# Recurrence gates with the two halves of the split input stacked over the rows of a 64-channel block: two products per block instead of three per gate

## The chip, the cores and the metric

The kernel runs on one core of a Trainium2 chip. The metric is the device time of one execution in microseconds (us), the median of several runs. TensorE multiplies matrices: a product (MATMUL) sends the columns of its moving operand through an array that holds the weights, and each product has a weight load (LDWEIGHTS) of its own ahead of it. ScalarE (ACT in the profile) does activations and casts, VectorE (DVE) the arithmetic on two operands, GpSimd (POOL) little here, SyncE (SP) issues DMAs. Each engine takes its instructions in the order of the program.

## The reference, cut to what matters

Two layers of a mixed backbone over 256 latent and 256 context tokens, with three token mixers in each layer, a merge by gates and an MLP. The change lies in the first mixer, a bidirectional gated linear recurrence whose two gates are products with block-diagonal weights (eight blocks of 64 channels):

```python
xc = centred_depthwise_conv(x_in, conv_w, conv_b).astype(F32)
xb = xc.reshape(B, T, LRU_BLOCKS, LRU_BLOCK)              # 8 blocks of 64
r = sigmoid(einsum('btni,dnio->dbtno', xb, wa) + ba)      # d: two directions
i = sigmoid(einsum('btni,dnio->dbtno', xb, wx) + bx)
log_a = -LRU_C * r * softplus(-lam)
a = exp(log_a)
b = sqrt(-expm1(2.0 * log_a)) * (i * xc)
hf = linear_scan(a[0], b[0], h0f, False)
hb = linear_scan(a[1], b[1], h0b, True)
y = (hf + hb) * gelu(gate_in)
```

## The kernel before

Activations are held feature-major: 128 channels in the partitions, up to 512 tokens in the columns. Every float32 product is made from three products in the type float32r: weights and input are split into a rounded high part and a low rest (`split`, L223: a copy on ScalarE, a subtraction on VectorE), and high times high, high times low and low times high are summed in PSUM. Nearly all of TensorE's work is such triples on streamed weights (`mm3`, L234, and L1027 to L1029 for the products called ptok). ScalarE and VectorE split each piece of weights (whi and wlo) ahead of its use, with four buffers each.

Between these streamed products, `Lanes` issues the steps of dependent chains: H (the second mixer, `hgrn`), A (attention), L (the recurrence, `lru`), N (norms) and X (modulation). A step is what a chain does up to its next `yield`; the numbers that it yields (VectorE's time and a delay) decide when the next step is issued. The tile framework's scheduler then lays the issued work out on each engine, and the result is a fixed order of instructions per engine.

`lru` runs once for each of four heads j (128 channels, so two blocks of 64) in each of two layers: eight times. It splits the gates' weights (gw into lw) and the convolved input (xc into lx), then for each direction d makes the two gates: `pr` (recurrence gate, its tanh into rr) and `pi` (input gate, its tanh into iis). The weights of one gate and direction are one 128x128 matrix with the two 64x64 blocks on its diagonal and zeros elsewhere. A gate is three products of 128 rows, 128 columns of weights and 512 tokens (L847), so `lru` has 12 products, and the kernel 96. Each gate's PSUM tile is of the tag "L", which has one buffer: the next gate's first product waits until the tanh has read the last one.

The other tiles that the text names are lv (products of the second mixer within blocks, L547), sc (attention scores, L746, where two heads of 64 rows each lie side by side in the array), tp (transposes, L793), pav (attention output, L812), pg (the merge's gates, through `mm3`), PT, s and sog (results on ScalarE of the attention and of the second mixer's output gate), ge (the gelu of the recurrence's other branch).

Of the kernel before, what the change touches and what calls it, by code (L numbers as in the profile page):

```python
# [10 lines left out]
F32 = mybir.dt.float32  # L11
# [5 lines left out]
ALU = mybir.AluOpType  # L17
# [39 lines left out]
def merge_order(l):  # L57
    # some gates first, while the mixers' chains end
    count = {}
    for part in MERGE[l].split():  # L60
        bi = int(part[0])
        for what in part[1:]:
            i = count.get((bi, what), 0)
            count[bi, what] = i + 1
            yield bi, BRANCH_ORDER[bi], {"g": "gate", "p": "proj"}[what], i
# [35 lines left out]
class Piece:  # L101
    """Products with streamed weights: body(weights) yields after each run of products."""
# [5 lines left out]
class Lanes:  # L108
    """Chains of dependent steps that are issued between the runs of products.

    A step yields the time that the vector engine needs for what it issued, and how many runs more the chain waits."""
# [43 lines left out]
def hybrid_kernel(  # L155
# [67 lines left out]
    def split(hi, lo, src, scale=None, eng=nc.vector):  # L223
        # hi <- rounded part of scale * src, lo <- the rest
        if scale is None:
            nc.scalar.copy(hi, src)  # L226
            eng.tensor_tensor(out=lo, in0=src, in1=hi.bitcast(F32), op=ALU.subtract)  # L227
        else:
            nc.scalar.mul(hi, src, scale)
            nc.vector.scalar_tensor_tensor(  # L230
                out=lo, in0=src, scalar=scale, in1=hi.bitcast(F32), op0=ALU.mult, op1=ALU.subtract
            )
# [13 lines left out]
    def mm3_pairs(dsts, ws, x, nk, c0, c1):  # L246
        # two pieces at a time, so that x may still be arriving
# [15 lines left out]
    def layer_scalars():  # L263
# [13 lines left out]
        for l in range(DEPTH):  # L277
            # f = lb + (1 - lb) * (1 + tanh) / 2 as offset and slope
# [40 lines left out]
    def rope_tables(l):  # L319
        # ctab[:, cos|sin, tile, k|q, head, :], with the norm's gains and the scores' scale  # L320
# [8 lines left out]
    mod = [cpool.tile([P, 3, 2, 16], F32, name=f"mod{l}") for l in range(DEPTH)]  # L329

    def modulation_rows():
        # most sections, a row for each feature: the vector engine has time while the tensor engine is busy
# [34 lines left out]
    def last_modulation():  # L367
        # the last section: four groups of columns in four parts of the array
# [55 lines left out]
    def column_sums(parts, n, tag="A"):  # L424
        # sums over the features, one column for each 128 tokens
# [12 lines left out]
    def spread(r, n, tag="A"):  # L438
        # a row of n * 128 columns in every partition
# [14 lines left out]
    def modulated(u, r, a, b, k, s):  # L454
        # u = h * r * a + b in high and low parts
# [29 lines left out]
    def small_rstd(ss, n, temps):  # L485
        # 1 / sqrt(ss / n + eps) for a few columns: a first guess from the exponent, two steps
# [6 lines left out]
        # with x = v * r * r: r * (15 - 10 x + 3 x^2) / 8, but for the factor 3 / 8, then r * (3 - x) / 2 with that factor  # L493
# [14 lines left out]
    def first_half():  # L508
        # the latent stream's norm, before its products are issued
        q_ = lanes.lanes["N"]  # L510
        while len(q_) > 1 and lanes.step("N"):
            pass

# [1 line left out]
    def hgrn(l, j, TF, Q, vtok, sog, ys):  # L515
# [4 lines left out]
        # products over blocks, states of the context stream  # L520
# [9 lines left out]
        # within blocks of 64 tokens, the blocks of a tile side by side  # L530
# [7 lines left out]
        def place(b, src, shift):  # L538
            # blocks in the upper (b = 0) or the lower half of the partitions
# [13 lines left out]
        def mixed(t, hh, c0, n):  # L553
            # [first halves of slot 0 | second halves of slot 1] of the 2*hh blocks in columns c0..c0+n
# [17 lines left out]
        # A^T[s, t] of both directions, level by level  # L572
        Tt = TF[:]
        width = T2
        for lev in range(8):
# [11 lines left out]
            # widen the products to blocks of 2*hh  # L587
# [30 lines left out]
        # final states of the context stream  # L618
# [18 lines left out]
        # outputs, token-major  # L637
# [34 lines left out]
    def attention(l, j, qk, vtok, bias, ys):  # L672
        Tq = T2 if l == 0 else TL
        misc = two_k("misc")
        # normalised keys and queries, token-major: [k | q] of two heads for each 128 tokens
# [23 lines left out]
        # rotary embedding of the latent tokens  # L699
# [48 lines left out]
        def softmax(qt, sc):  # L748
            # both heads at once
# [55 lines left out]
        def applied(qt):  # L805
            # both heads at once, in two parts of the array
# [28 lines left out]
    def lru(l, j, xc, ge, gw, ys):  # L835
# [6 lines left out]
        split(*xs, xc)  # L842
        yield 1.2, 0

        def product(dst, i):
            for n, (a, b) in enumerate(((0, 0), (0, 1), (1, 0))):
                nc.tensor.matmul(dst, lhsT=ws[a][:, i, :], rhs=xs[b], start=(n == 0), stop=(n == 2))  # L847
        for d in range(2):
            c = 2 * j + d
            pr_ = psum("L", "pr")  # L850
            product(pr_, 2 * d)
            nc.scalar.activation(rr[:, d], pr_, AF.Tanh, bias=hb[l][0][:, c:c + 1], scale=0.5)
            yield
            pi_ = psum("L", "pi")
            product(pi_, 2 * d + 1)
            nc.scalar.activation(iis[d], pi_, AF.Tanh, bias=hb[l][1][:, c:c + 1], scale=0.5)
# [37 lines left out]
    def fin_query(Tq, Q, p_):  # L894
        # twice the silu
# [5 lines left out]
    def fin_outgate(l, Tq, sog, p_):  # L901
        # the gain over four times (1 + tanh)
# [17 lines left out]
    def fin_gelu(Tq, ge, p_):  # L920
        # twice the tanh GeLU
# [12 lines left out]
    def mixer_pieces(l):  # L934
        T = T2 if l == 0 else TL
        heads = []
        for j in range(4):
# [9 lines left out]
            def opened(nm, m=m, j=j):  # L947
                # tiles of a chain, when its first piece begins
# [9 lines left out]
                if nm == "tok":  # L958
                    m.bias = four_k("bias", (4, TL))
                    (nc.gpsimd if l or j else nc.sync).dma_start(out=m.bias, in_=biasd[l, j])  # L960
                    # [v of both mixers | k and q], two blocks of tokens each
# [28 lines left out]
            def group(ws, m=m, opened=opened, closed=closed):  # L990
                # the first products, while the modulation arrives
# [70 lines left out]
    def merge_pieces(l):  # L1062
# [7 lines left out]
        def gate_tile(bi, d):  # L1070
            # several gates in a tile
# [78 lines left out]
    def down_pieces(l, kind, sub, x, section, T, finished, after, pre=None):  # L1150
        # pieces d = 0..7 into the residual; with after, the last four by streams, so that a norm can start early
# [119 lines left out]
    def start():  # L1271
# [51 lines left out]
        def busy(n):  # L1323
            # keeps the tensor engine's clock up while the first data arrive
# [30 lines left out]
        def arrive():  # L1355
            # what the products of the first chunk need
# [11 lines left out]
        def later():  # L1368
            # what the products of the first chunks don't need
# [11 lines left out]
        def ahead(k, n):  # L1381
            # within the products of chunk k, what those of chunk k + 2 need
# [24 lines left out]
    # weights run ahead of the pieces that use them  # L1407
# [24 lines left out]
def _lay(inputs):  # L1432
# [42 lines left out]
    for l in range(DEPTH):  # L1475
        for nm, v in (
# [4 lines left out]
            ("bx", f["lru_bx"][l].reshape(2, 4, P).transpose(2, 1, 0).reshape(P, 8)),  # L1481
# [10 lines left out]
    lw = np.zeros((DEPTH, 4, P, 2, 2, P), np.float32)  # L1492
    for gi, nm in enumerate(("lru_wa", "lru_wx")):
        w = f[nm].reshape(DEPTH, 2, 4, 2, 64, 64)
        for b in range(2):
            lw[:, :, b * 64:(b + 1) * 64, :, gi, b * 64:(b + 1) * 64] = w[:, :, :, b].transpose(0, 2, 3, 1, 4)
# [65 lines left out]
```

## Time and profile before

| what | value |
|---|---|
| time, median of 3 runs | 1529.8 us (1528.32 to 1531.29) |
| span of the profiled execution, first to last instruction | 1526.3 us |
| TensorE busy | 1513.7 us (99%) |
| VectorE busy | 1115.9 us (73%) |
| ScalarE busy | 735.0 us (48%) |
| TensorE's granted clock, mean | 0.999 |

The profiled execution's own time is not listed apart from its span; the median of the runs is 3.5 us above that span. The busy time of an engine counts the time in which at least one of its instructions was in flight, so that overlapping products are not counted twice.

### The profile page before, as it was taken

What the parts mean: (1) busy time and instruction counts of PE and PEld (TensorE: products, weight loads), DVE (VectorE), ACT (ScalarE), POOL (GpSimd) and SP (SyncE); (2) the same over time, 40 slices, a digit from 0 to 9 for tenths busy, and PEclk for the clock granted to TensorE, in tenths of its full rate; (3) what the DMA queues carried; (4) which work ended last, traced back from release to release, by engine and by line L of the source; (5) the groups of instructions that cost most, each with busy time, mean ns of one, the idle gap of its engine ahead of it and who ended that gap; (6) DMA issues with size and microseconds to landing.
All of it is one profiled execution on the core that took longest, in us unless ns stands there. A gap on an engine that the chain in (4) does not pass through costs nothing.

```text
span 1526.3 us, 24145 instructions
## 1 busy us (share of the span) xinstructions
PE 1513.7 (99%) x9554; PEld 1300.8 (85%) x9554; DVE 1115.9 (73%) x2118; ACT 735.0 (48%) x1229; POOL 26.4 (2%) x57
## 2 busy tenths in 40 slices
PE   9999999999999999999999999999999999999999
PEld 4778788878888889888888889888888899999999
DVE  6776768586478898988685856778787856776664
ACT  3457575666333333532322323475766854454442
POOL 0200000020000000000000000000000000000000
PEclk9999999999999999999999999999999999999999
DMA  9413122221273562445463532313313345755553
GB/s 368 146 53 104 56 90 70 70 77 62 91 250 136 187 240 70 171 174 206 139 220 127 204 126 82 133 63 126 104 70 105 109 167 182 274 167 184 186 183 125
DMA packets 61793, 217.36 MB, mean 142 GB/s; under 512 B 7792, under 2 KB 9456, under 8 KB 61680
## 3 DMA queue, kind: packets, MB, share of 16 engines
q1 hardware_dynamic: 59328, 209.88, 39.5%
q0 software_dynamic: 1648, 5.77, 1.2%
q8 instruction: 75, 1.23, 0.3%
q14 instruction: 38, 0.31, 0.1%
q10 hardware_dynamic: 704, 0.17, 0.1%
HBM read 214.74 MB, written 1.05 MB: 141 GB/s over the span
## 4 chain that ended last, share of the span: by engine, by line
PE 96%; DVE 2%; ACT 1%; issue 1%; DMA 0%; SPq 0%; DVEq 0%
PE pd L240 7%; PE pd L242 7%; PE pd L241 7%; PE pf L242 5%; PE pf L240 5%; PE pf L241 5%; PE pg L240 5%; PE pg L241 4%; PE pg L242 4%; PE ptok L1027 3%; PE ptok L1029 3%; PE ptok L1028 3%; PE lv L547 2%; PE pp L241 2%; PE pp L240 2%; PE pp L242 2%
## 5 line engine op out<-in xcount | busy, mean ns | idle before, releaser
L226 ACT CAST whi<-raw 128x1024 fp32r<-128x1024 f32 x296 | 310.3, 1050 | 477.0 <-PE pd L241 157.2
L227 DVE TENSOR_TENSOR wlo<-raw,whi 128x1024 fp32r<-128x1024 f32 x295 | 360.3, 1223 | 151.2 <-ACT whi L226 149.4
L242 PE MATMUL pd<-hhi,wlo 128*128 128x256 f32 (+1 forms) x544 | 177.8, 327 | 0.0
L240 PE MATMUL pd<-hhi,whi 128*128 128x256 f32 (+1 forms) x544 | 177.8, 327 | 0.0
L241 PE MATMUL pd<-hlo,whi 128*128 128x256 f32 (+1 forms) x544 | 177.7, 327 | 0.0
L354 DVE CUSTOM_DVE_ANT_0 junk<-arow,crow 128x1024 bf16<-128x1024 f32 x144 | 173.3, 1219 | 2.2 <-DMA arow<-in_adaw 2.0
L241 PE MATMUL pf<-xlo,whi 128*128 128x256 f32 (+1 forms) x464 | 155.0, 334 | 0.0
L242 PE MATMUL pf<-xhi,wlo 128*128 128x256 f32 (+1 forms) x464 | 155.0, 334 | 0.0
L240 PE MATMUL pf<-xhi,whi 128*128 128x256 f32 (+1 forms) x464 | 155.0, 334 | 0.0
L240 PE MATMUL pg<-xhi,whi 128*128 128x512 f32 (+1 forms) x384 | 131.5, 342 | 0.0
L241 PE MATMUL pg<-xlo,whi 128*128 128x512 f32 (+1 forms) x384 | 129.2, 336 | 0.0
L242 PE MATMUL pg<-xhi,wlo 128*128 128x512 f32 (+1 forms) x384 | 129.2, 336 | 0.0
L1145 DVE SCALAR_TENSOR_TENSOR h<-pd,mod,h 128x256 f32<-128x256 f32 x120 | 54.9, 480 | 81.2 <-PE pd L242 79.2
L241 PEld LDWEIGHTS pd<-hlo,whi 128*128 128x128 f32 x544 | 103.5, 190 | 8.8
L240 PEld LDWEIGHTS pd<-hhi,whi 128*128 128x128 f32 x544 | 103.5, 190 | 8.8
L242 PEld LDWEIGHTS pd<-hhi,wlo 128*128 128x128 f32 x544 | 103.5, 190 | 8.6
L241 PEld LDWEIGHTS pf<-xlo,whi 128*128 128x128 f32 x464 | 88.1, 190 | 8.8
L242 PEld LDWEIGHTS pf<-xhi,wlo 128*128 128x128 f32 x464 | 88.1, 190 | 8.7
L240 PEld LDWEIGHTS pf<-xhi,whi 128*128 128x128 f32 x464 | 88.0, 190 | 8.7
L1027 PE MATMUL ptok<-whi,xhi 128*128 128x512 f32 (+1 forms) x224 | 87.4, 395 | 1.1 <-DVE h L1145 1.1
L1029 PE MATMUL ptok<-wlo,xhi 128*128 128x512 f32 (+1 forms) x224 | 84.4, 377 | 0.0
L1028 PE MATMUL ptok<-whi,xlo 128*128 128x512 f32 (+1 forms) x224 | 84.2, 376 | 0.2 <-DVE xlo L463 0.2
(329 smaller groups left out, 3240.0 us busy)
## 6 DMA issues: line engine op xcount, KB each, us to landing
raw<-in_wpack SPq DMA_DIRECT2D x296, 512.0 KB, 3.5
arow<-in_adaw SPq DMA_DIRECT2D x72, 512.0 KB, 4.7
a<-in_ada0w SPq DMA_DIRECT2D x16, 512.0 KB, 10.4
araw<-in_lastw SPq DMA_DIRECT2D x8, 512.0 KB, 6.3
bias<-in_biasd POOLq DMA_DIRECT2D x7, 512.0 KB, 4.3
h<-in_xT SPq DMA_DIRECT2D x4, 512.0 KB, 5.5
gw<-in_lruw POOLq DMA_DIRECT2D x8, 256.0 KB, 2.9
out<-h SPq DMA_DIRECT2D x8, 128.0 KB, 2.0
```

The costliest lines, as they stand in the source:

```text
L226: nc.scalar.copy(hi, src)
L227: eng.tensor_tensor(out=lo, in0=src, in1=hi.bitcast(F32), op=ALU.subtract)
L240: nc.tensor.matmul(d, lhsT=whi[:, k, :], rhs=xhi, start=(k == 0), stop=False)
L241: nc.tensor.matmul(d, lhsT=whi[:, k, :], rhs=xlo, start=False, stop=False)
L242: nc.tensor.matmul(d, lhsT=wlo[:, k, :], rhs=xhi, start=False, stop=(k == nk - 1))
L354: nc.vector.tensor_tensor_reduce(out=junk, in0=raw, in1=crow[s], scale=1.0, scalar=0.0, op0=ALU.mult, op1=ALU.add, accum_out=section_of(l, ...
L547: nc.tensor.matmul(dst, lhsT=lhs(b), rhs=rhs(b), start=True, stop=True)
L1027: nc.tensor.matmul(dst, lhsT=xhi[:, k, tsl], rhs=whi[:, kk, :], start=(k == 0), stop=False)
L1028: nc.tensor.matmul(dst, lhsT=xlo[:, k, tsl], rhs=whi[:, kk, :], start=False, stop=False)
L1029: nc.tensor.matmul(dst, lhsT=xhi[:, k, tsl], rhs=wlo[:, kk, :], start=False, stop=(k == KD - 1))
L1145: nc.vector.scalar_tensor_tensor(out=h[:, d, sl], in0=p_[:, sl], scalar=mods(l, section, s)[:, d:d + 1], in1=h[:, d, sl], op0=ALU.mult, op ...
```

## The change

The input is no longer split into one tile of high parts and one of low parts. For each block b of 64 channels there is now one tile: the high part in the block's own 64 rows, the low part in the other 64 rows. The weights are laid out on the host so that one 128x128 matrix serves one block and direction: both gates side by side in its 128 columns, and the same 64 rows of weights twice, over the high and over the low input. A first product (128 rows) then gives high weights times high input plus high weights times low input for both gates of the block; a second one (64 rows, only the block's own half) adds low weights times high input. That is two products per block and direction instead of three per gate and direction: 8 in a call of `lru` instead of 12, and 64 in the kernel instead of 96. The two gates of a block lie in the two halves of the PSUM tile's partitions, and each half is read by a tanh of its own (64 partitions, 512 columns), so there are four tanh per direction instead of two. The split of the input is two copies and two subtractions on 64 partitions instead of one of each on 128. The bias of the input gate is rolled by 64 channels on the host. The first step yields 1.8 instead of 1.2. The bytes that are loaded are the same.

```diff
         split(*ws, gw)
-        split(*xs, xc)
-        yield 1.2, 0
-
-        def product(dst, i):
-            for n, (a, b) in enumerate(((0, 0), (0, 1), (1, 0))):
-                nc.tensor.matmul(dst, lhsT=ws[a][:, i, :], rhs=xs[b], start=(n == 0), stop=(n == 2))
+
+        half = [slice(HB * b, HB * (b + 1)) for b in range(2)]
+        for b in range(2):
+            own, other = half[b], half[1 - b]
+            nc.scalar.copy(xs[b][own], xc[own])
+            nc.vector.tensor_tensor(out=xs[b][other], in0=xc[own], in1=xs[b][own].bitcast(F32), op=ALU.subtract)
+        yield 1.8, 0
+
+        def product(dst, d, b):
+
+            own = half[b]
+            nc.tensor.matmul(dst, lhsT=ws[0][:, 2 * d + b, :], rhs=xs[b], start=True, stop=False)
+            nc.tensor.matmul(dst, lhsT=ws[1][own, 2 * d + b, :], rhs=xs[b][own], start=False, stop=True)
+
         for d in range(2):
             c = 2 * j + d
-            pr_ = psum("L", "pr")
-            product(pr_, 2 * d)
-            nc.scalar.activation(rr[:, d], pr_, AF.Tanh, bias=hb[l][0][:, c:c + 1], scale=0.5)
-            yield
-            pi_ = psum("L", "pi")
-            product(pi_, 2 * d + 1)
-            nc.scalar.activation(iis[d], pi_, AF.Tanh, bias=hb[l][1][:, c:c + 1], scale=0.5)
+            for b in range(2):
+                own, other = half[b], half[1 - b]
+                pg_ = psum("L", "pri")
+                product(pg_, d, b)
+                nc.scalar.activation(rr[own, d], pg_[own], AF.Tanh, bias=hb[l][0][own, c:c + 1], scale=0.5)
+                nc.scalar.activation(iis[d][own], pg_[other], AF.Tanh, bias=hb[l][1][other, c:c + 1], scale=0.5)
+                if b == 0:
+                    yield
...
-            ("bx", f["lru_bx"][l].reshape(2, 4, P).transpose(2, 1, 0).reshape(P, 8)),
+            ("bx", np.roll(f["lru_bx"][l].reshape(2, 4, P).transpose(2, 1, 0).reshape(P, 8), 64, 0)),
...
-    lw = np.zeros((DEPTH, 4, P, 2, 2, P), np.float32)
+    lw = np.empty((DEPTH, 4, 2, 64, 2, 2, 2, 64), np.float32)
     for gi, nm in enumerate(("lru_wa", "lru_wx")):
         w = f[nm].reshape(DEPTH, 2, 4, 2, 64, 64)
         for b in range(2):
-            lw[:, :, b * 64:(b + 1) * 64, :, gi, b * 64:(b + 1) * 64] = w[:, :, :, b].transpose(0, 2, 3, 1, 4)
+            lw[:, :, :, :, :, b, gi ^ b, :] = w[:, :, :, b].transpose(0, 2, 3, 1, 4)[:, :, None]
     a["lruw"] = lw.reshape(DEPTH, 4, P, 4, P)
```

The lines of the changed kernel are numbered differently: its first product is L853, the second (64 rows) L854, its tanh L862 and L863, and what was L1027 to L1029 (ptok) is L1036 to L1038.

The first place is on TensorE, where the second head of layer 0 makes its first gate product; ptok are the streamed products around it, sc the attention scores. Before:

```order
L1029 MATMUL ptok<-wlo,xhi 128x512
L746 MATMUL sc<-rotT 128x256 x6
L746 MATMUL sc<-kcT,qT 128x256 x6
L847 MATMUL pr<-lx,lw 128x512 x3
L1027 MATMUL ptok<-whi,xhi 128x512
L1028 MATMUL ptok<-whi,xlo 128x512
```

Now:

```order
L1038 MATMUL ptok<-wlo,xhi 128x512
L746 MATMUL sc<-rotT 128x256 x6
L746 MATMUL sc<-kcT,qT 128x256 x6
L853 MATMUL pri<-lx,lw 128x512
L854 MATMUL pri<-lx,lw 128x512
L1036 MATMUL ptok<-whi,xhi 128x512
L1037 MATMUL ptok<-whi,xlo 128x512
```

The triple has become a pair at the same place, and the second of the pair, whose weights have 64 rows, stands between two products of 128 rows.

The second place is on TensorE in layer 1, where the same chain meets the second mixer's lv. Before, the pr of one direction:

```order
L1029 MATMUL ptok<-wlo,xhi 128x512
L547 MATMUL lv<-QQ,km 64x64 x4
L847 MATMUL pr<-lx,lw 128x512 x3
L1028 MATMUL ptok<-whi,xlo 128x512
L1029 MATMUL ptok<-wlo,xhi 128x512
```

Now, eight streamed products further on, the pair that takes its place:

```order
L1038 MATMUL ptok<-wlo,xhi 128x512
L853 MATMUL pri<-lx,lw 128x512
L854 MATMUL pri<-lx,lw 128x512
L547 MATMUL lv<-QQ,km 64x64 x4
L793 MATMUL tp<-con,s 128x128 x8
```

The pair moved behind other streamed products, and here lv follows the second product directly.

The third place is on ScalarE, in the last head of layer 0, where whi is a cast of streamed weights. Before, from the first gate's tanh (L852) on:

```order
L852 ACTIVATE lr<-pr,hba 128x512
L769 ACTIVATE s<-s,misc 128x512 x2
L797 COPY PT<-tp 128x4x128
L903 ACTIVATE sog<-pog 128x512
L797 COPY PT<-tp 128x4x128
L904 ACTIVATE sog<-sog,hg_653 128x512
L226 CAST whi<-raw 128x1024
L1086 ACTIVATE gt<-pg 128x512
```

Now:

```order
L862 ACTIVATE lr<-pri,hba 64x512
L769 ACTIVATE s<-s,misc 128x512 x2
L797 COPY PT<-tp 128x4x128
L912 ACTIVATE sog<-pog 128x512
L797 COPY PT<-tp 128x4x128
L913 ACTIVATE sog<-sog,hg_653 128x512
L226 CAST whi<-raw 128x1024
L863 ACTIVATE li<-pri,hbx 64x512
L862 ACTIVATE lr<-pri,hba 64x512
L863 ACTIVATE li<-pri,hbx 64x512
```

The PSUM tile of the first block is now read by two tanh, and seven other instructions stand between the first (L862) and the second (L863), after which alone the tile is free.

## Rows read from the trace of the kernel before

**Rows 1.** The page's part 1: busy us, share of the span, instructions.

```profile
PE 1513.7 (99%) x9554; PEld 1300.8 (85%) x9554; DVE 1115.9 (73%) x2118; ACT 735.0 (48%) x1229; POOL 26.4 (2%) x57
```

**Rows 2.** The page's part 4: the chain that ended last, by engine.

```profile
PE 96%; DVE 2%; ACT 1%; issue 1%; DMA 0%; SPq 0%; DVEq 0%
```

**Rows 3.** Waits of TensorE: us in total, times, longest us; longest of nine rows.

```profile
PE pf L253 <- ACT xhi L462: 2.7, 3, 1.1
```

**Rows 4.** Groups by form, TensorE: array shape, operand; busy us, mean ns; idle before.

```profile
L547 PE MATMUL lv<-QQ,km 128*64 128x64 f32 x576 | 29.0, 235 | 0.0
...
L847 PE MATMUL pi<-lx,lw 128*128 128x512 f32 x48 | 14.9, 412 | 0.0
L847 PE MATMUL pr<-lx,lw 128*128 128x512 f32 x48 | 14.3, 407 | 0.0
...
L746 PE MATMUL sc<-kcT,qT 64*128 64x256 f32 x144 | 12.7, 284 | 0.0
```

**Rows 5.** Timeline of TensorE's products, 97 to 103 us: start, us, instruction.

```profile
96.99 0.40 PE L1029 MATMUL ptok<-wlo,xhi 128*128 128x512 f32 x1
97.31 0.62 PE L746 MATMUL sc<-rotT 64*128 64x256 f32 x6
97.77 0.52 PE L746 MATMUL sc<-kcT,qT 64*128 64x256 f32 x6
98.22 0.96 PE L847 MATMUL pr<-lx,lw 128*128 128x512 f32 x3
99.02 0.40 PE L1027 MATMUL ptok<-whi,xhi 128*128 128x512 f32 x1
...
101.53 0.39 PE L1029 MATMUL ptok<-wlo,xhi 128*128 128x512 f32 x1
101.84 0.69 PE L547 MATMUL lv<-QQ,km 128*64 128x64 f32 x16
102.46 0.50 PE L1027 MATMUL ptok<-whi,xhi 128*128 128x512 f32 x1
102.79 0.39 PE L1028 MATMUL ptok<-whi,xlo 128*128 128x512 f32 x1
```

**Rows 6.** Timeline of TensorE's weight loads, 97 to 99 us; idle before in brackets.

```profile
97.31 0.42 PEld L746 LDWEIGHTS sc<-rotT 64*128 64x128 f32 x6 [0.36 <-issue]
...
98.22 0.53 PEld L847 LDWEIGHTS pr<-lx,lw 128*128 128x128 f32 x3
...
99.03 0.19 PEld L1028 LDWEIGHTS ptok<-whi,xlo 128*128 128x128 f32 x1
```

**Rows 7.** Timeline of TensorE's products, 1198 to 1200 us.

```profile
1198.21 0.38 PE L240 MATMUL pg<-xhi,whi 128*128 128x256 f32 x1
1198.53 0.62 PE L746 MATMUL sc<-rotT 64*128 64x256 f32 x3
...
1199.43 0.39 PE L241 MATMUL pg<-xlo,whi 128*128 128x256 f32 x1
1199.65 0.28 PE L242 MATMUL pg<-xhi,wlo 128*128 128x256 f32 x1
1199.77 0.28 PE L240 MATMUL pg<-xhi,whi 128*128 128x256 f32 x1
```

**Rows 8.** Groups by form, ScalarE: busy us, mean ns; idle before and what ended it.

```profile
L226 ACT CAST whi<-raw 128x1024 fp32r<-128x1024 f32 x296 | 310.3, 1050 | 477.0 <-PE pd L241 157.2 <-issue 86.1 <-PE pg L241 64.2
...
L226 ACT CAST hhi<-rl 128x256 fp32r<-128x256 f32 x32 | 12.9, 404 | 16.8 <-DVE rl L1209 16.8
L852 ACT ACTIVATE lr<-pr,hba 128x512 f32<-128x512 f32 x16 | 11.1, 691 | 12.1 <-PE pr L847 12.1
...
L226 ACT CAST lx<-xc 128x512 fp32r<-128x512 f32 x8 | 5.0, 629 | 0.0
...
L542 ACT COPY At<-lv 64x256 f32<-64x256 f32 x8 | 3.0, 369 | 0.4 <-PE lv L547 0.3
```

**Rows 9.** Groups by form, VectorE: busy us, mean ns; idle before.

```profile
L227 DVE TENSOR_TENSOR lx<-xc,lx 128x512 fp32r<-128x512 f32 x8 | 5.5, 684 | 0.0
```

**Rows 10.** Busy time by stretch: PE, PEld, DVE, ACT, POOL; clock; DMA share; GB/s.

```profile
1200.00:1210.00 10.00, 10.00 (x87) 9.17 (x85) 8.00 (x19) 9.59 (x18) 0.00 (x0) 1.00 0.24 81
...
1220.00:1230.00 10.00, 10.00 (x86) 10.00 (x86) 7.69 (x12) 4.58 (x7) 0.00 (x0) 1.00 0.59 201
```

## The prediction

> **What bounds the kernel now.** I read the busy times first: TensorE is busy for 1513.7 of 1526.3 us, VectorE for 73% and ScalarE for 48% of them [rows 1]. The chain that ended last says the same in another way: 96% of it are TensorE's products [rows 2]. TensorE's own list of waits has nine rows, of which the longest sums to 2.7 us, and none of them is a gate product of the recurrence [rows 3]; what waits there is ScalarE, 12.1 us for pr [rows 8]. So what the change does to the time is, to a first order, what it does to the sum of the intervals between TensorE's products. The other engines count only where they become later than the product that needs them.
>
> A busy time per instruction is of no use for such a sum, since products overlap: the groups give 407 and 412 ns for one pr or pi [rows 4]. What counts is the interval from start to start. Twelve streamed products of 128 rows and 512 columns start between 99.02 and 101.53 us, eleven intervals, so 0.228 us each [rows 5].
>
> The second thing to see is the array's shape, which the profile prints ahead of the operands: the gates are `128*128`, lv is `128*64`, sc is `64*128` [rows 4]. Where the shape changes, two things lengthen. The last product before the change takes 0.32 us to the next start (96.99 to 97.31) in place of 0.228, that is 0.09 more; the three pr behind sc take 0.80 us (98.22 to 99.02) in place of 0.68, that is 0.12 more. The same shows around lv: 0.31 on the way in (101.53 to 101.84), 0.33 for the first product on the way out (102.46 to 102.79) [rows 5]. The weight loads say where the second part comes from. Within one shape a load runs under the product before it: the load for the product that starts at 99.25 starts at 99.03, with the product of 99.02. At a change the load starts only with its own product, at 97.31 and at 98.22, and the loading unit sat idle for 0.36 us ahead of the first of them [rows 6].
>
> **The change part by part.**
>
> *Products removed.* 96 become 64, all with 512 columns. 32 x 0.228 = 7.3 us less. That the second product of a pair has 64 rows saves nothing more: its 512 columns pass all the same. Twelve sc in two groups, two heads side by side, take 0.91 us (97.31 to 98.22) [rows 5]; less 0.21 for the change of shape on either side that lies within, six pairs of 256 columns take 0.117 us each, which is what a 128-row product of 256 columns takes (0.12 us, 1199.65 to 1199.77 [rows 7]).
>
> *Changes of shape added.* The second product of each pair has 64 rows of weights, as sc has, so I take it to run in sc's shape. Between two 128-row products it costs a change in and a change out. I counted the shapes along TensorE's whole order: 201 changes before, 257 after. Of the 32 pairs 27 stand as at the first place shown, with two changes more each; two are followed by sc and add none, three by lv as at the second place and add one each; the rest is moved blocks. So 56 more. Their price is 0.09 + 0.12 = 0.21 us from the rows at pr, with the same 512 columns. The nearest single case is one pg between two groups of sc: it takes 0.32 us (1198.21 to 1198.53) where its neighbours take 0.12, so 0.20 for one load that shows and one end that is waited for; the product behind sc takes 0.22 (1199.43 to 1199.65) [rows 7]. Around lv it is 0.18. I take 0.21, since it comes from the products in question: 56 x 0.21 = 11.8 us more. The ends are 56 x 0.18 = 10.1 and 11.8.
>
> The Trainium skill states the rule in "TensorEngine Tiling (Array Packing)", section "Key Properties": changing the tiling mode, not just the tile, drains TensorE. The trace agrees on the drain (0.09 us), but shows a second part that the sentence doesn't name, the load that can't run ahead (0.12 us). By the drain alone the sum would be 56 x 0.09 = 5.0 us against 7.3.
>
> *ScalarE's work.* 32 tanh become 64, and 8 casts of lx become 16. On ScalarE 64 partitions cost what 128 do: 369 ns for a copy of 64x256, 404 ns for a cast of 128x256. So 32 x 0.69 + 8 x 0.63 = 27 us more on ScalarE [rows 8]; the bound below, if half the partitions took half the time, is nothing. TensorE's products cover it, as long as the streamed weights' casts stay ahead. ScalarE waits 477 us in total ahead of those casts, mostly for TensorE to free a buffer [rows 8]; even where it is fullest (9.59 of 10 us at 1200 to 1210) it is down at 4.58 by 1220 to 1230 [rows 10]. A head adds 3.4 us there, against four buffers of weights, each some 24 products of 0.12 us. I count it at nothing; without that cover it would cost up to 3.4 us in the last head.
>
> *VectorE's work.* 8 subtractions become 16: 8 x 0.68 = 5.5 us [rows 9]. It lies beside 1513.7 us of products; the first pair needs only the first of the two subtractions, which ends when the one subtraction ended. Nothing, or 0.3 to 0.7 us for a head where it is late.
>
> *The one PSUM buffer.* The next pair waits for two tanh, not one. That is at least 0.69 us later, and in the third place shown seven other instructions of ScalarE, at 0.6 to 1.05 us each, so 5 to 6 us, stand between the two tanh. Between these two pairs TensorE has 19 products of 0.228, sc (0.91), lv and tp: 6 to 7 us. So ScalarE and TensorE arrive there about together. Behind a waiting pair stand the streamed products of all chains, so such a wait goes straight into the time. Elsewhere I find 3 to 8 us of products between two pairs of a head and 1.4 to 5.3 us of ScalarE's work. I take nothing, with up to 1 us in each of some six narrow places as the upper bound.
>
> *What moves.* The larger yield (1.8) and the new waits shift tp, lv and sc by a few products; that is in the count of changes, and nothing else of it is on TensorE's path.
>
> The sum on the profiled execution: 1526.3 - 7.3 + 11.8 = 1530.8 us of span. The runs' median lies 3.5 us above that execution's span, so 1534.3 us, 0.3% more than 1529.8. (A difference of 0.2%, 3.1 us, is about what a measurement of this kernel can tell from none.)
>
> **The rivals.**
>
> *The changes cost nothing here (faster).* If the 64-row product's weights were loaded under the first product of the pair, and nothing were drained, only the removed products count: 1529.8 - 7.3 = 1522.5 us. For it: both products of a pair write the same tile and read the same rows, and a load within one shape does run ahead. Against: no change of shape in the rows comes without both parts. It decides where a change costs less than 7.3 / 56 = 0.13 us.
>
> *Only one of the two parts is paid (the same).* The drain alone gives 56 x 0.09 = 5.0, the load alone 56 x 0.12 = 6.7 us: 1527.5 to 1529.2. For it: a 64-row load may be lighter than those behind sc, whose heads alternate. Against: the single pg paid both. That rule of the skill, taken literally, lies here.
>
> *ScalarE comes too late (slower still).* The two tanh, with other work between, hold the one buffer: 1 us in ten of the 24 intervals within heads gives 10 us, so 1544 us; 6 us give 1540. For it: 9.59 of 10 us busy [rows 10], and the third place. Against: ScalarE waited for pr, not the reverse [rows 8].
>
> **How the numbers follow.** Forecast 0.62 (1532.6 to 1538, by 0.18 to 0.21 us for a change and up to 4 us of waits), free changes 0.12, one part 0.13, late ScalarE 0.13 (1538 to 1546). The range from 1527.5 to 1540 takes in the forecast, one part, and the nearer half of the late ScalarE; it leaves out free changes and the far half. Slower by over 0.2% (above 1532.9): nearly nine tenths of the forecast and all of the late ScalarE, 0.68. Within 0.2%: one part and the forecast's lower end, 0.20. Faster: 0.12.
>
> **What would show it.** pri at L854 should stand as `64*128`; the interval from L853 to L854 should be 0.32, from L854 to the next 0.43 (0.228 + 0.12 + 0.09), and the next product's 0.34. TensorE's idle rows should show no new wait for L862 or L863 above 1 us, ScalarE's busy time should be about 762 us and VectorE's 1121. The prediction is wrong if L854's load runs ahead under L853, if TensorE waits for li at L863 in several heads, or if the streamed weights' casts come late.

## The result and the profile after

The changed kernel takes 1536.65 us (median of 5 runs, 1535.63 to 1541.99) against 1529.8 (1527.92 to 1531.33) of the kernel before, run beside it: ratio 1.0053, 95% interval 1.0037 to 1.007. It is slower by half a per cent. Where TensorE's mean granted clock was 1.000 (2.4 GHz), the changed kernel takes 1535.63 to 1536.65 us (3 runs) and the kernel before 1525.94 to 1527.26 (21 runs, beside the experiments below): some 9 us apart rather than 6.9. The forecast was 1534.3, with 1527.5 to 1540 as its range; the span of the profiled execution is 1534.9 us where 1530.8 was forecast and 1526.3 was measured before.

The page's part 1 (busy us, share of the span, instructions) and the first line of its part 4 (the chain that ended last, by engine), to be read beside [rows 1, 2]:

```profile
PE 1520.8 (99%) x9522; PEld 1294.1 (84%) x9522; DVE 1120.1 (73%) x2126; ACT 762.1 (50%) x1269; POOL 26.5 (2%) x57
...
PE 93%; DVE 4%; ACT 1%; issue 1%; DMA 1%; SPq 0%; DVEq 0%; ACTq 0%
```

There are 32 products fewer, as the change says, and TensorE is nevertheless busy for 7.1 us more. ScalarE has 27 us more and VectorE 4. The chain is still TensorE's, but VectorE's share of it went from 2% to 4%.

The first place of the change on TensorE's timeline (start, us, instruction), which answers to [rows 5]:

```profile
96.98 0.50 PE L853 MATMUL pri<-lx,lw 128*128 128x512 f32 x1
97.41 0.50 PE L854 MATMUL pri<-lx,lw 64*128 64x512 f32 x1
97.84 0.50 PE L1036 MATMUL ptok<-whi,xhi 128*128 128x512 f32 x1
98.18 0.40 PE L1037 MATMUL ptok<-whi,xlo 128*128 128x512 f32 x1
98.42 0.39 PE L1038 MATMUL ptok<-wlo,xhi 128*128 128x512 f32 x1
...
99.33 0.39 PE L1036 MATMUL ptok<-whi,xhi 128*128 128x512 f32 x1
99.56 0.39 PE L1037 MATMUL ptok<-whi,xlo 128*128 128x512 f32 x1
```

L854 stands as `64*128`. From its start to the next product 0.43 us pass, from that product to the one behind it 0.34, and between products of one shape 0.23. (L853 takes 0.43 here, since it comes behind sc and pays the entry of that change too.) The weight loads at the same place, with the idle time before them in brackets, answer to [rows 6]:

```profile
96.98 0.19 PEld L853 LDWEIGHTS pri<-lx,lw 128*128 128x128 f32 x1
97.41 0.18 PEld L854 LDWEIGHTS pri<-lx,lw 64*128 64x128 f32 x1 [0.25 <-issue]
97.84 0.19 PEld L1036 LDWEIGHTS ptok<-whi,xhi 128*128 128x128 f32 x1 [0.25 <-issue]
97.95 0.19 PEld L1037 LDWEIGHTS ptok<-whi,xlo 128*128 128x128 f32 x1
```

The loads at 97.41 and 97.84 start only with their own products; the one at 97.95, within a shape, runs under the product before it. It is so at every change of shape: at all 257 of them the load starts less than 0.01 us ahead of its product. Over all 32 pairs the loading unit's list of waits says the same (us in total, times, longest):

```profile
PEld pri L854 <- issue: 9.3, 32, 0.4
PEld ptok L1036 <- issue: 6.5, 24, 0.4
```

Before, there were 5 such waits of 1.9 us at the first product of a triple of ptok, and none at the gates. Over the program, the median interval from a 128-row product to L854 is 0.327 us, from L854 on 0.426, and the product behind it takes 0.336: together 0.41 more than three products of one shape, so 0.20 for a change where [rows 5] gave 0.21.

What the forecast did not have is in TensorE's list of waits (us in total, times, longest), beside [rows 3]:

```profile
PE tp L793 <- ACT s L785: 0.9, 1, 0.9
...
PE pri L853 <- ACT li L863: 0.3, 1, 0.3
PE kt L623 <- DVE At L615: 0.2, 1, 0.2
...
PE ptok L1038 <- DVE wlo L227: 0.2, 1, 0.2
```

None of these four stood there before. The one that the forecast feared (L853 behind the tanh of L863) is 0.3 us, once. From the first gate product to the last product of the program 9.8 us more pass than before (the stretch ahead of it, which the change doesn't touch, was 1.2 us shorter in this execution, so the span grew by 8.6). Of these 4.5 are the forecast's products and changes of shape, and some 5.3 are such waits. Counted from start to start, the four places come to 2.8 us: tp 1.1, pri and kt 0.4 each, and L1038 0.3 in each of three heads, of which the list has one. The rest is spread over short intervals that I haven't followed.

### The profile page after: what moved, and what is told of

It is laid out like the page before. It is cut to its first block, busy times and chain, and to the rows that moved or that the text cites. A ratio compares the mean times of both kernels' runs of the same rounds, so it can differ in the third digit from the quotient of the medians.

```text
span 1534.9 us, 24127 instructions
## 1 busy us (share of the span) xinstructions
PE 1520.8 (99%) x9522; PEld 1294.1 (84%) x9522; DVE 1120.1 (73%) x2126; ACT 762.1 (50%) x1269; POOL 26.5 (2%) x57
## 4 chain that ended last, share of the span: by engine, by line
PE 93%; DVE 4%; ACT 1%; issue 1%; DMA 1%; SPq 0%; DVEq 0%; ACTq 0%
PE pd L240 7%; PE pd L242 7%; PE pd L241 7%; PE pf L240 5%; PE pf L242 5%; PE pf L241 5%; PE pg L240 4%; PE pg L241 4%; PE pg L242 4%; PE ptok L1036 3%; PE ptok L1038 3%; PE ptok L1037 3%; PE pp L241 2%; PE pp L242 2%; PE pp L240 2%; PE lv L547 2%
## 5 line engine op out<-in xcount | busy, mean ns | idle before, releaser
L1036 PE MATMUL ptok<-whi,xhi 128*128 128x512 f32 (+1 forms) x224 | 89.6, 404 | 1.1 <-DVE h L1154 1.1
L1038 PE MATMUL ptok<-wlo,xhi 128*128 128x512 f32 (+1 forms) x224 | 85.0, 379 | 0.4 <-DVE wlo L227 0.2
L1037 PE MATMUL ptok<-whi,xlo 128*128 128x512 f32 (+1 forms) x224 | 84.8, 379 | 0.2 <-DVE xlo L463 0.2
```

The costliest lines, as they stand in the source:

```text
L1036: nc.tensor.matmul(dst, lhsT=xhi[:, k, tsl], rhs=whi[:, kk, :], start=(k == 0), stop=False)
L1037: nc.tensor.matmul(dst, lhsT=xlo[:, k, tsl], rhs=whi[:, kk, :], start=False, stop=False)
L1038: nc.tensor.matmul(dst, lhsT=xhi[:, k, tsl], rhs=wlo[:, kk, :], start=False, stop=(k == KD - 1))
```

## The experiments

The 12 kernels below were each run in five rounds beside the kernel before, whose medians beside them were 1527.7 to 1528.1 us. "us more" and "us less" are worked out from the ratio, on 1528. "Loss beyond shape" is the measured difference less what the products (0.228 each) and the counted changes of shape (0.21 each) give. The 95% intervals reach 1.5 to 2 us to either side, so a loss below 2 us can't be told from none.

### One suspected cost alone: the shape

**e3_third_64**, the kernel before, with only the third product of each triple on 64 rows (the other rows' low weights are left out):

```diff
-                nc.tensor.matmul(dst, lhsT=ws[a][:, i, :], rhs=xs[b], start=(n == 0), stop=(n == 2))
+                rows = slice(0, HB if n == 2 else P)
+                nc.tensor.matmul(dst, lhsT=ws[a][rows, i, :], rhs=xs[b][rows], start=(n == 0), stop=(n == 2))
```

> The kernel before, but the third product of each gate (low weights times high input) takes only 64 of its 128 rows, so that one block's low weights are left out. 96 gate products, nothing changed on ScalarE and VectorE, 259 changes of shape for 201. Theory: 58 x 0.21 = 12.2 us more, 1542.0 us. Rival, a change that follows the gates' products is cheap because tile and rows stay the same (half the price): 1535.9 us. Rival, changes cost nothing: 1529.8 us.

1539.87 us (1537.76 to 1541.71), ratio 1.0079 (1.0065 to 1.0092), 12.1 us more. There are 259 changes of shape, 58 more than before: 58 x 0.21 = 12.2. Less work in every third product, the same number of products, the same ScalarE, and the price of the shape: by the interval 9.9 to 14.1 us, so 0.17 to 0.24 for a change.

**e1_full_rows**, the changed kernel with the second product on all 128 rows:

```diff
-            nc.tensor.matmul(dst, lhsT=ws[1][own, 2 * d + b, :], rhs=xs[b][own], start=False, stop=True)
+            nc.tensor.matmul(dst, lhsT=ws[1][:, 2 * d + b, :], rhs=xs[b], start=False, stop=True)
```

> The changed kernel, but the second product of a pair takes all 128 rows (low weights over both halves of the stacked input; the added low-times-low part is part of the exact product), so no product of the gates has 64 rows. 64 gate products as in the changed kernel, 200 changes of shape (257 with 64 rows, 201 before). Theory (a change of shape costs 0.21 us, the rest of the loss is waits for ScalarE and VectorE, which stay as they are): 57 x 0.21 = 12.0 us below the changed kernel, so about 1524.7 us, and still 2 to 4 us above 1522.5. Rival, the 64-row product itself is what makes the rest of the loss: 1522.5 us. Rival, changes of shape are cheap and the loss is ScalarE's: 1530 us or more.

1531.99 us (1530.43 to 1536.93), ratio 1.0032 (1.0022 to 1.0042). A miss: the shapes are gone (200 changes), yet it is 4.9 us slower than before where 7.5 less was due, so 12.4 are lost elsewhere. (Its time lies where the rival with cheap changes of shape put it, but e3 has ruled that out.) Its list of waits has TensorE's

```profile
PE ptok L1038 <- DVE wlo L227: 1.7, 3, 0.6
...
PE tp L793 <- ACT s L785: 1.3, 1, 1.3
...
PE tp L793 <- ACT s L769: 1.0, 3, 0.3
...
PE pav L814 <- ACT PTc L800: 0.3, 1, 0.3
```

The waits of the changed kernel for s and for wlo are here too, and larger; that for li is as long as there, that of kt is not in the list, and two rows are new. So the changes of shape had hidden a second loss: a TensorE that is held up by them comes later to where it would have waited.

### Whose work is the second loss?

**e2_halves**, the kernel before with its split and its tanh in halves of 64 partitions:

```diff
-        split(*xs, xc)
+        half = [slice(HB * b, HB * (b + 1)) for b in range(2)]
+        for own in half:
+            nc.scalar.copy(xs[0][own], xc[own])
+            nc.vector.tensor_tensor(out=xs[1][own], in0=xc[own], in1=xs[0][own].bitcast(F32), op=ALU.subtract)
...
-            nc.scalar.activation(rr[:, d], pr_, AF.Tanh, bias=hb[l][0][:, c:c + 1], scale=0.5)
+            for own in half:
+                nc.scalar.activation(rr[own, d], pr_[own], AF.Tanh, bias=hb[l][0][own, c:c + 1], scale=0.5)
```

> The kernel before with its 96 products of 128 rows, but each tanh of a gate and each step of the input's split is done in two halves of 64 partitions, as in the changed kernel: ScalarE's and VectorE's added work alone. The scheduler moves other blocks by it: 219 changes of shape for 201. Theory (ScalarE's and VectorE's added work makes waits of 2 to 4 us): 1529.8 + 18 x 0.21 + 2 to 4 = 1535.6 to 1537.6 us. Rival (that work is hidden): 1529.8 + 3.8 = 1533.6 us by the moved blocks alone, or 1530 if those don't count either. ScalarE busy 762 us by either.

1534.4 us (1534.2 to 1538.01), ratio 1.0051 (1.0038 to 1.0063), 7.8 us more. The 219 changes of shape, 18 more, are 3.8 of them; 4.0 are lost beyond shape, with the products untouched.

**e4_yield**, the changed kernel with the first step's number as before:

```diff
-        yield 1.8, 0
+        yield 1.2, 0
```

> The changed kernel with the old yield of 1.2 in place of 1.8, so that the lanes step as before. 262 changes of shape for 257. Theory: the yield matters only through the order; 5 x 0.21 = 1 us more than the changed kernel, 1537.7 us, and the waits stay. Rival, the larger yield is what pushed consumers against their producers: 2 to 4 us less than the changed kernel, about 1533.5 us.

1535.94 us (1535.38 to 1540.13), ratio 1.006 (1.0048 to 1.0073). Nothing is gained; the number in the yield isn't the cause.

**e10_whole_tanh**, the changed kernel with split and tanh on whole partitions again. The gates are then of mixed data, which leaves out the sorting of the two gates; **e11_full_rows_whole_tanh** is the same on e1, with full rows:

```diff
-        for b in range(2):
-            own, other = half[b], half[1 - b]
-            nc.scalar.copy(xs[b][own], xc[own])
-            nc.vector.tensor_tensor(out=xs[b][other], in0=xc[own], in1=xs[b][own].bitcast(F32), op=ALU.subtract)
-        yield 1.8, 0
+        split(*xs, xc)
+        yield 1.2, 0
...
-                nc.scalar.activation(rr[own, d], pg_[own], AF.Tanh, bias=hb[l][0][own, c:c + 1], scale=0.5)
-                nc.scalar.activation(iis[d][own], pg_[other], AF.Tanh, bias=hb[l][1][other, c:c + 1], scale=0.5)
+                nc.scalar.activation(iis[d] if b else rr[:, d], pg_, AF.Tanh, bias=hb[l][b][:, c:c + 1], scale=0.5)
```

> The changed kernel's 64 gate products, 64-row ones included, with the split of the input and the tanh on 128 partitions as before: one tanh per pair, so ScalarE and VectorE do what they did before. Left out: the stacking of the input and the sorting of the two gates, so the gates are computed from mixed data; only the time counts. 261 changes of shape for 201. Theory (what is lost beyond the changes of shape is waits for ScalarE's added work): 60 x 0.21 - 7.3 = 5.3 us above the kernel before. Rival (the order and the pairs themselves make those waits): 8 to 10 us above, as the changed kernel is.

> Second products of 128 rows, and the split of the input and the tanh on 128 partitions as before: ScalarE and VectorE as before, 64 products in place of 96, 201 changes of shape as before. Left out: the stacking and the sorting of the gates, as in the run beside it. Theory (ScalarE's added work is what keeps the kernel with full rows 4.9 us above the kernel before in place of 7.3 below): 7.3 us below the kernel before. Rival (in these stretches the products are not the bound at all, other engines are, so that fewer products only wait longer): 0 to 2 us below.

e10: 1532.82 us (1531.38 to 1536.16), ratio 1.0029 (1.0019 to 1.0038), 4.4 us more; products and 261 changes of shape give 5.3. e11: 1520.97 us (1519.14 to 1522.61), ratio 0.9946 (0.9934 to 0.9959), 8.2 us less; the products give 7.3. In neither is anything lost beyond shape, and the four waits shown for e1 are gone from e11's list. The second loss belongs to what these two leave out: the halves, with the sorting of the two gates.

**e14_extra_act**, e11 with one more tanh on ScalarE after each gate's, which reads the convolved input and whose output nobody reads (mixed data as in e11):

```diff
+                nc.scalar.activation(dm[own], xc[own], AF.Tanh, scale=0.5)
```

> The kernel with full rows and whole tanh (the gates are then of mixed data, so work is left out), with one more tanh of 64x512 on ScalarE after each gate's tanh, which reads the convolved input and writes a tile that nothing reads: 32 x 0.69 = 22 us of ScalarE as in the version with full rows, but the gate's PSUM tile is free after the first tanh. Changes of shape 199. Theory (the amount of ScalarE's work costs): 1527 to 1531 us, against 1521.0 without the added tanh. Rival (the second tanh costs because it holds the one PSUM buffer): 1520 to 1523.

1521.05 us (1519.27 to 1523.43), ratio 0.9958 (0.9946 to 0.9969): 1.3 lost of the 13 between e1 and e11, which can't be told from none. ScalarE is busy for 751.0 us here against 733.6 in e11 and 761.8 in e1. So it isn't the amount of ScalarE's work, which I had held it to be. (Nothing waits for these tanh. That the tanh of the gates cost because others wait for them would fit, but no run shows it.)

**e15_late_r**, e11 with the two tanh of a direction writing each other's tile, so that the recurrence gate is complete one product later, as in every whole computation with stacked products (mixed data as in e11):

```diff
-                nc.scalar.activation(iis[d] if b else rr[:, d], pg_, AF.Tanh, bias=hb[l][b][:, c:c + 1], scale=0.5)
+                nc.scalar.activation(rr[:, d] if b else iis[d], pg_, AF.Tanh, bias=hb[l][b][:, c:c + 1], scale=0.5)
```

> The version with full rows and whole tanh (the gates are of mixed data, so work is left out), with the two tanh of a direction writing each other's tile: the recurrence gate's tile is now complete only after the second product's tanh, as it is in every whole computation with stacked products, where before and in the version without this edit the first tanh completes it, and the two activations that follow from it (ltau, and the exponential) can run before the second product. Instructions, durations and ScalarE's total stay the same, no tanh is added, each PSUM tile is free after one tanh. Changes of shape 204 instead of 201. Theory L (what the stacked products lose beyond their changes of shape is that the recurrence gate is complete one product later, which bunches ScalarE's work behind it): 1526 to 1531 us against 1521.0. Theory H (it is the one PSUM buffer, held by two tanh, or the input's split in halves): 1520 to 1523, of which 3 x 0.21 = 0.6 are changes of shape.

1521.71 us (1521.48 to 1526.39), ratio 0.9964 (0.9952 to 0.9976): 5.5 less than before, so 1.2 lost beyond shape, again within the noise. This alone isn't it either.

### Ways to do the halves' work elsewhere

**e6_casts_dve** and **e7_casts_pool** are e1 with the 16 casts of lx on VectorE or on GpSimd:

```diff
-            nc.scalar.copy(xs[b][own], xc[own])
+            nc.vector.tensor_copy(xs[b][own], xc[own])
```

> Full rows, stacking and tanh in halves as in the kernel with full rows, but the 16 casts of the input are done on VectorE: 16 x 0.63 = 10 us less on ScalarE, more on VectorE. Theory (ScalarE's added work makes the waits): of the 12 us of waits some third goes, 3 to 4 us less than with the casts on ScalarE, about 1 us above the kernel before. Rival (VectorE's chain is as late): no difference, 5 us above.

> As the run beside it, with the 16 casts on GpSimd, which does little here, at perhaps 1 to 2 us each. Theory: ScalarE and VectorE are both relieved, so this is the best of the versions with full rows, 1 us above to 2 us below the kernel before. Rival (the casts are not what is waited for): 5 us above.

e6: 1531.25 us (1529.74 to 1534.51), ratio 1.0022 (1.0012 to 1.0032). e7: 1532.7 us (1530.35 to 1536.37), ratio 1.0026 (1.0016 to 1.0036). Both miss what was expected of them (about 1 us above the kernel before, and 1 above to 2 below): they are 3.4 and 4.0 above. Ten to eleven are lost beyond shape in both; the engine of these casts hardly matters.

**e12_pool_moves** and **e13_dve_moves** are whole computations with one cast and one tanh of 128 partitions each, as before, and copies of 64x512 (on GpSimd, or on VectorE) that bring the halves to their places; the biases are laid out to suit:

```diff
+        nc.scalar.copy(xs[0], xc)
+        nc.gpsimd.tensor_copy(xs[1][half[1]], xs[0][half[1]])
+        nc.vector.tensor_tensor(out=xs[1][half[0]], in0=xc[half[1]], in1=xs[1][half[1]].bitcast(F32), op=ALU.subtract)
+        nc.vector.tensor_tensor(out=xs[0][half[1]], in0=xc[half[0]], in1=xs[0][half[0]].bitcast(F32), op=ALU.subtract)
...
+                nc.scalar.activation(tau[:, d] if b else rr[:, d], pg_, AF.Tanh, bias=hb[l][b][:, c:c + 1], scale=0.5)
+                if b == 0:
+                    nc.gpsimd.tensor_copy(iis[d][own], rr[other, d])
+                else:
+                    nc.gpsimd.tensor_copy(rr[own, d], tau[own, d])
+                    nc.gpsimd.tensor_copy(iis[d][own], tau[other, d])
+                yield
```

> A whole computation again: the 64 stacked products with full rows, one tanh of 128 partitions per product as in the kernel before (32 in all), the input's cast whole on ScalarE (8), and the halves brought to their partitions by 56 copies of 64x512 on GpSimd, which is idle but for 26 us. ScalarE has exactly the work of the kernel before, VectorE 8 half subtractions more. Changes of shape 219 instead of 201. Theory (what the changed kernel loses beyond its changes of shape is the 32 added tanh on ScalarE): 32 x 0.228 = 7.3 less, 18 x 0.21 = 3.8 more, waits nothing, so 1524 to 1526 us against 1528 to 1530 of the kernel before, ratio 0.997 to 0.998. Rival A (it is the partition layout or the step's length that costs, whoever does the work): 1529 to 1533. Rival B (GpSimd's copies slow VectorE, which shares in the waits): above 1531.

> The same with the 56 copies of 64x512 on VectorE instead of GpSimd, some 56 x 0.4 to 0.7 = 22 to 39 us more on VectorE; changes of shape 216. Theory (ScalarE alone was late): 1523 to 1525 us, ratio 0.997. Rival (VectorE's work costs as ScalarE's does, since both are nearly full in the mixers' stretches): 1528 to 1534.

e12: 1534.98 us (1532.74 to 1537.1), ratio 1.0047 (1.0036 to 1.0059). e13: 1535.14 us (1531.88 to 1536.84), ratio 1.0045 (1.0033 to 1.0057). Both miss by 10 us. (e12 lies where its rival B had it, that GpSimd's copies slow VectorE; e13 has no such copies and takes as long.) ScalarE's busy time is back at 733 us in e12, and still 10.7 us are lost beyond shape. No whole computation with stacked products came out faster than the kernel before.

### One place accounted for

In three of layer 1's four heads one wait can be followed through all versions: the product L1038 that needs wlo. VectorE works almost without a gap from ge on (L934; L930 in e11), through the subtractions of lx, to this wlo. The changed kernel (start, us, instruction):

```profile
1003.97 0.43 DVE L934 SCALAR_TENSOR_TENSOR ge<-ge,gpre 128x256 f32<-128x256 f32 x1
...
1005.71 1.40 DVE L847 TENSOR_TENSOR lx<-xc,lx 64x512 fp32r<-64x512 f32 x2
...
1009.71 1.22 DVE L227 TENSOR_TENSOR wlo<-raw,whi 128x1024 fp32r<-128x1024 f32 x1
```

And e11, with whole partitions:

```profile
996.67 0.42 DVE L930 SCALAR_TENSOR_TENSOR ge<-ge,gpre 128x256 f32<-128x256 f32 x1
...
998.29 0.68 DVE L227 TENSOR_TENSOR lx<-xc,lx 128x512 fp32r<-128x512 f32 x1
...
1001.44 1.22 DVE L227 TENSOR_TENSOR wlo<-raw,whi 128x1024 fp32r<-128x1024 f32 x1
```

From ge to the end of wlo 6.96 us pass in the one and 5.99 in the other (before: 5.99 too). The second subtraction is 0.72 of the 0.97, and two gaps of 0.1 us, ahead of the two and behind the reduction that follows them, are most of the rest. The product at the end of this, in the changed kernel's timeline of TensorE:

```profile
1010.24 0.39 PE L1036 MATMUL ptok<-whi,xhi 128*128 128x512 f32 x1
1010.47 0.39 PE L1037 MATMUL ptok<-whi,xlo 128*128 128x512 f32 x1
1010.98 0.50 PE L1038 MATMUL ptok<-wlo,xhi 128*128 128x512 f32 x1
```

wlo ends at 1010.93, and L1038 starts 0.51 us behind L1037 in place of 0.23: a wait of 0.28. In the kernel before:

```profile
1004.84 1.22 DVE L227 TENSOR_TENSOR wlo<-raw,whi 128x1024 fp32r<-128x1024 f32 x1
...
1006.78 0.62 PE L1027 MATMUL ptok<-whi,xhi 128*128 128x512 f32 x2
1007.23 0.39 PE L1028 MATMUL ptok<-whi,xlo 128*128 128x512 f32 x1
1007.46 0.39 PE L1029 MATMUL ptok<-wlo,xhi 128*128 128x512 f32 x1
```

Here wlo ends at 1006.06, 1.40 us ahead of its product, L1029. Two L1027 stand in a row: the first product of the next triple lies ahead of that L1029, which is so in this version and in e3 alone of those in the table. Without its 0.23 the margin is 1.17 us, and the table counts from that (e3's is 2.20 as it stands). Three things change the margin: each gate product that no longer stands ahead of this place on TensorE takes 0.228 off it, each change of shape adds 0.21, and the second subtraction, with the two gaps, takes off 0.97. Six gate products stood there before; four stand there in e10 and e11, two in e15, e1 and the changed kernel, whose second pair has moved behind the place.

| version | worked out | margin measured, or wait (negative) |
|---|---|---|
| e3 (4 changes more) | 1.17 + 0.84 = 2.01 | 1.97 |
| e2 (halves, 0.95 there; TensorE held up, 0.41) | 1.17 - 0.95 + 0.41 = 0.63 | 0.62 to 0.66 |
| e10 (2 products fewer, 4 changes) | 1.17 - 0.46 + 0.84 = 1.55 | 1.60 |
| e11 (2 fewer) | 1.17 - 0.46 = 0.71 | 0.72 |
| e15 (4 fewer) | 1.17 - 0.91 = 0.26 | 0.26 |
| changed kernel (4 fewer, 2 changes, halves) | 1.17 - 0.91 + 0.42 - 0.97 = -0.29 | -0.28 |
| e1 (4 fewer, halves) | 1.17 - 0.91 - 0.97 = -0.71 | -0.72 |

All come out within 0.05. In e2 TensorE was itself held up ahead of the place: its first pi product starts 0.51 us behind the L1033 before it (1006.33 to 1006.84) in place of 0.23, just behind the second tanh of pr (which ends at 1006.79), and the three pi take 0.13 more. This is the second loss at work in one place: what is taken off TensorE is taken off the cover of VectorE's work, and the halves add to that work. It comes to 0.3 us in each of three heads of the changed kernel, and to 0.7 in e1. The longest single wait of the changed kernel, tp's for s, is of the attention's chain, which runs through the same two engines:

```profile
286.01 0.17 DVE L781 RECIPROCAL misc<-misc 128x4 f32<-128x4 f32 x1
...
286.22 1.71 ACT L785 ACTIVATE s<-s,misc 128x256 f32<-128x256 f32 x4 [1.02 <-DVE misc L781]
...
286.78 0.44 PE L793 MATMUL tp<-con,s 128*128 128x128 f32 x2 [0.92 <-ACT s L785]
```

ScalarE stood idle for 1.02 us here until VectorE had made a reciprocal, so it was VectorE that came late. What made it late I haven't followed, nor the other waits of tp and those of pav.

What stays open: e6, e7, e12 and e13 wait in other places (e6 for km on VectorE in front of lv, 2.2 us; e12 for sog on ScalarE in front of ptok, 1.7), and lose as much. Split in halves is what e1, e6, e7, e12 and e13 share and e10, e11, e14 and e15 lack. But they also share the 1.8 of the first step (which made no difference in e4), and no run has the split in halves alone. The hold on the one PSUM buffer by two tanh wasn't run by itself either. It shows in the waits of pri for li (0.3 us in the changed kernel, 1.1 over three heads in e4) and in pi's wait in e2, but it isn't needed for the loss: in e12 and e13 one tanh frees the buffer, and they lose as much.

## Why the prediction was right, and where it was off

*Products removed and changes of shape.* Right, mechanism and size. 96 became 64, 201 changes became 257, and each costs the load that can't run ahead and the end that is waited for, 0.20 to 0.21 us together; e3 gives 12.1 us for 58, and the margins in the table fit at the same price. The rule in the Trainium skill, "TensorEngine Tiling (Array Packing)", section "Key Properties", that a change of mode drains TensorE agrees with the 0.09 us on the way in, but by the drain alone e3 would have lost 5.2 us, not 12.1. So the rivals "the changes cost nothing" and "only one part is paid" are out: the price is above 0.13, and both parts show in the loads.

*ScalarE's and VectorE's work.* The sizes were right: ScalarE is busy for 762.1 us (762 forecast), VectorE for 1120.1 (1121). These are the rows that answer to [rows 8, 9] (busy us, mean ns, idle before and what ended it):

```profile
L862 ACT ACTIVATE lr<-pri,hba 64x512 f32<-64x512 f32 x32 | 21.9, 684 | 19.3 <-PE pri L854 18.9
L863 ACT ACTIVATE li<-pri,hbx 64x512 f32<-64x512 f32 x32 | 21.9, 683 | 1.2 <-PE tp L793 0.6
L846 ACT CAST lx<-xc 64x512 fp32r<-64x512 f32 x16 | 9.9, 618 | 0.4 <-DVE lw L227 0.2
```

```profile
L847 DVE TENSOR_TENSOR lx<-xc,lx 64x512 fp32r<-64x512 f32 x16 | 11.0, 686 | 0.5
```

Half the partitions take the whole time. What failed is the step that put this work at nothing in the sum: "I count it at nothing" for ScalarE, and for VectorE "Nothing, or 0.3 to 0.7 us for a head where it is late". The alternative in the second sentence is what happened at wlo: 0.3 us in three heads. All that is lost beyond products and shape comes to some 5 us from the first gate product on (9.8 less 4.5), 4.1 of the span and 2.4 of the medians (6.9 less 4.5). The forecast's own lines allowed "up to 4 us of waits", but its sum had none. That the medians come so close to the forecast is in part luck: the kernel before ran some 3 us slower beside this run than at a granted clock of 1.000, where the two lie some 9 us apart, over 4 more than products and shape give. I had read the cover from totals (477 us that ScalarE waits ahead of the casts) and not from the margin of a single wlo, 1.40 us, which the trace of before already showed.

*The one PSUM buffer.* As taken: L853 waits for L863 once, for 0.3 us, at the third place that was shown. The rival "ScalarE comes too late" was right that late work of the other engines costs time, but had it in the wrong place: it is mostly streamed products and transposes that wait, not the next pair, and in the two places followed here VectorE is what came late. It isn't 10 us here, in part since the changes of shape give cover (0.42 us at the place of the table). In e1, without them, the loss beyond shape is 12.4.

*What moves.* Put at nothing, which was wrong at one place. The second pair moved behind the place of the table, and so 0.46 us less of TensorE's work covered the wlo there; the next triple's product that moved behind it took another 0.23.

## What to carry to other kernels

A product on part of the array's rows between products on all of them costs two changes of shape, here 0.42 us where the product itself takes 0.23: pad it to full rows with zeros or with rows that do no harm (e1: 1531.99 us against 1536.65), or gather such products so that they share a change (not run here). When work is taken off the engine that bounds a kernel, the same time is taken off the cover of every other engine; before counting added work elsewhere as hidden, look up the margin in microseconds between the end of each tile that the bound engine needs and the product that needs it, not the other engine's idle total. An operation on half the partitions cost ScalarE and VectorE here the time of a whole one (683 against 691 ns, 686 against 684), so a layout that must be put together from halves pays twice.

## What was unexpected of the hardware

The price of a change of shape is paid by a 64-row load as by any other: the loads of L854 take 0.18 us where those of 128 rows take 0.19, and neither runs under a product of the other shape. And 32 added tanh of 0.63 us on ScalarE (e14), on a kernel whose ScalarE was at 48%, moved the time by about 0.1%, while one half subtraction more on VectorE put 0.97 us on the way to a wlo that had a margin of 1.40.
